# Hybrid conv / mLSTM / GLA trunk: three VectorE instructions placed behind the second head's key step

## The chip, the cores and the metric

The kernel runs on one core of one Trainium2 chip. The metric is device time in microseconds (us). The core has TensorE (PE) for matrix products, VectorE (DVE) and ScalarE (ACT) for elementwise work, GpSimd (POOL), and SyncE (SP), whose queue issues the DMAs here. Each engine works through its own list of instructions in order; a semaphore holds an instruction until what it reads is there.

## The reference

A trunk of two residual layers on a 1024 x 1024 activation (sequence x width), each followed by a dense SwiGLU, with a final RMSNorm. The change lies in the first layer's mixer, which is a causal 31-tap convolution module and a four-head mLSTM side by side:

```python
def conv_mlstm_mixer(h, w_in, conv_w, conv_b, ln_g, ln_b, qk_conv_w, qk_conv_b, gate_b, head_g, w_out):
    z = h @ w_in
    ca, cg, q, k, v, og, gates = jnp.split(z, cuts, -1)
    u = causal_depthwise_conv(ca * sigmoid(cg), conv_w, conv_b)     # 31 taps, 512 channels
    u = silu(layernorm(u, ln_g, ln_b))                              # over the 512 channels
    qk = silu(causal_depthwise_conv(concat([q, k]), qk_conv_w, qk_conv_b))   # 4 taps
    hm = mlstm_chunkwise(q, k, v, i_pre, f_pre)                     # 4 heads of 128
    hm = head_rmsnorm(hm * sigmoid(og), head_g)
    return concat([u, hm]) @ w_out

# one chunk of a head:
    S = (qc @ kc.T) * exp(logD - m_t)
    num = S @ vc + w_inter * (qc @ C);  den = S.sum(-1) + w_inter * (qc @ n)
    wk = exp(g - m_new) * kc
    C = decay * C + wk.T @ vc;  n = decay * n + wk.sum(-2)
```

The change touches the mean of `layernorm` over the convolution's output `u`, and the step `wk` of the second head.

## The kernel before

Activations lie feature-major, as eight tiles of 128 features by 512 positions for each half of the sequence. Every large product is done in three passes of TensorE: each fp32 operand is split into a high part, which ScalarE writes as a rounded copy (`wH`, `hH`), and a low part, which VectorE writes as the difference (`wL`, `hL`, line 168 for a mixer's weights); `mm3` (lines 174 to 176) then adds low x high, high x low and high x high into one PSUM bank. So a weight block of 128 x 1024 costs one DMA from SP (line 164, into one of two `raw` buffers), one ScalarE copy (line 167) and one VectorE subtraction (line 168). Without the last one its products can't start, and its `raw` buffer doesn't come free.

The first mixer is written as a list of steps, `ORDER0`. What matters here is its middle: `v3` (the fourth convolution), `a1a` and `x1a` (the second head's first half, prepared and mixed), `l` (layer norm), `g2` (value and output-gate products of the third head), `q2` (its query and key products).

- `conv(3)` ends with two VectorE additions (line 418) that take two convolution results `xy_289` and `xy_290` out of PSUM.
- `head_pre(1, 0)` is `a1a`. TensorE forms keys x queries (line 601) and transposes the keys (line 606). VectorE multiplies the scores by the decay, `rb` (line 612), scales the queries (line 613) and writes the weighted keys `kw` (line 615).
- `head_mix(1, 0)` is `x1a`. For each pair of chunks TensorE multiplies `kw` by the values (line 633), `rb` by the values (line 634) and, from the second chunk on, the queries by the running state `st` (line 636). VectorE writes that state: the first chunk's is a copy (line 639), the later ones are line 642. Then come the denominators (lines 647 to 649) and the division (line 652).
- `layer_norm()` adds the eight convolution tiles one after the other into `s` (line 434 once, line 436 six times), folds `s` in three shorter additions (line 428) and has TensorE average it with a matrix of constants (line 429). The rest of the norm takes that mean off all eight tiles (line 441), squares, sums, averages again and scales.
- `head_vo(2)` is `g2`: eight products per head, one per 128 positions, into banks `mm_2512`, `mm_2539`, `mm_2566` and so on, 24 matmuls of 256 columns each. VectorE takes the value half out (line 560) and ScalarE the gate half (line 561).
- `q2` is the loop's `"q"` branch. It asks for two weight blocks; the first one's low part is `wL_2733`.

The steps are not run in the order they are written. A planner keeps only the dependences, a priority for each instruction (`high_priority` moves weights and loads ahead) and its own estimate of each duration, and from these it sets one fixed order for each engine's list. The helper `behind(a, b)` gives the planner one more dependence: `a` may not stand ahead of `b`. It carries no semaphore, so on one engine it moves places in a list and adds no wait of its own. `made` holds the two instructions, high copy and low subtraction, of the weight block that was asked for last.

Of the kernel before, what the change touches and what calls it, by code (L numbers as in the profile page):

```python
# [13 lines left out]
ALU = mybir.AluOpType  # L14
PSUM = bass.MemoryType.PSUM

P = 128
# [64 lines left out]
def trunk_kernel(ctx, tc, xT, cols, gate_b0, ev_vo0, ev_u, ev_cw, ev_out, od_v0, od_u, od_out, gate_w2, fin_row,  # L82
                 w13, w2, out, xsp, rowd, ud, zd, ad, x1, cd, cv, td, vd, yd, bd, md):
    nc = tc.nc
    PE, ACT, DVE, POOL, SP = nc.tensor, nc.scalar, nc.vector, nc.gpsimd, nc.sync
# [10 lines left out]
    def nm(s):  # L96
        uid[0] += 1
        return f"{s}_{uid[0]}"

    def bank(tag):  # L100
        return ps.tile([P, 512], F32, tag=tag, name=nm(tag))

    def tmp(dt=F32):
        return tp.tile([P, HALF], dt, tag="t", name=nm("t"))
# [47 lines left out]
    def behind(ins, other):  # L152

        tc.add_manual_dep(ins.ins, other.ins.name, mybir.DependencyInfo(mybir.DependencyClass.NoSync, mybir.DependencyReason.DATA))


    made = []

    def weights(src, n, lo, off=WOFF, pool=None):

        own = {} if pool is None else {"bufs": 1}
        with tc.high_priority(offset=off):
            raw = wp.tile([P, 1088], F32, tag="raw", name=nm("raw"), bufs=2)[:, :n]
            SP.dma_start(raw, src)
            hi = (pool or wp).tile([P, 1088 if pool is None else n], F32R, tag="wH", name=nm("wH"), **own)[:, :n]
            low = (pool or wp).tile([P, 1088 if pool is None else n], F32R, tag="wL", name=nm("wL"), **own)[:, :n]
            first = ACT.activation(hi, raw, AF.Copy)
            cuts = lo.tensor_tensor(out=low, in0=raw, in1=hi, op=ALU.subtract)  # L168
        made[:] = first, cuts
        return hi, low  # L170
# [123 lines left out]
    def mixer0(cut, then):  # L294
        with tc.tile_pool(name="m0", bufs=1, reuse_waits="tile") as mp:
# [6 lines left out]
            def nextw(lo):  # L302
                return ready.pop(0) if ready else weights(ev_u[next(unit)], 1024, lo)
# [117 lines left out]
            Y = []  # L421

            def by_phase(t):
                return t.rearrange("p (e n) -> p e n", e=GT)

            def mean(b, s):
                for n in (4 * NT, 2 * NT, NT):
                    DVE.tensor_tensor(out=s[:, :n], in0=s[:, :n], in1=s[:, n:2 * n], op=ALU.add)
                PE.matmul(b, ones_p, s[:, :NT], start=True, stop=True)

            def layer_norm():

                s = tp.tile([P, HALF], F32, tag="s", name=nm("s"), bufs=1)
                DVE.tensor_tensor(out=s, in0=Y[0], in1=Y[1], op=ALU.add)
                for y in Y[2:]:
                    DVE.tensor_tensor(out=s, in0=s, in1=y, op=ALU.add)
                mu = bank("sm")[:, :NT]
                mean(mu, s)
                s = tp.tile([P, HALF], F32, tag="s", name=nm("s"), bufs=1)
                for j, y in enumerate(Y):  # L440
                    DVE.tensor_tensor(out=by_phase(y), in0=by_phase(y), in1=mu.unsqueeze(1).to_broadcast([P, GT, NT]),
                                      op=ALU.subtract)
                    t = tmp() if j else s
                    ACT.activation(t, y, AF.Square)
                    if j:
                        DVE.tensor_tensor(out=s, in0=s, in1=t, op=ALU.add)
                var = bank("sm")[:, :NT]
                mean(var, s)
                r = tp.tile([P, HALF], F32, tag="r", name=nm("r"), bufs=1)[:, :NT]
                rsqrt(r, var)  # L450
                for j, y in enumerate(Y):
                    DVE.tensor_tensor(out=by_phase(y), in0=by_phase(y), in1=r.unsqueeze(1).to_broadcast([P, GT, NT]), op=ALU.mult)
                    for e in range(0, GT, 4):
                        SP.dma_start(zd[GT * j + e:GT * j + e + 4].rearrange("e c a n -> (c a) e n"), by_phase(y)[:, e:e + 4])
# [14 lines left out]

                split(d, features[k, half], DVE, after)  # L470

            gcols = {}

            def gates(gz):

# [114 lines left out]
            def head_pre(hd, half, q, k):  # L590

                rb = mp.tile([P, HALF], F32, tag="bc0", name=nm("rb"), bufs=2)
                wb = mp.tile([P, HALF], F32, tag="bc1", name=nm("wb"), bufs=2)
                hs = slice(half * HALF, (half + 1) * HALF)
                SP.dma_start(rb, rowd[0, hd, hs].partition_broadcast(P))
                SP.dma_start(wb, rowd[1, hd, hs].partition_broadcast(P))
                cc, wk = gcols["c"], gcols["wk"]
                sb = bank("sm")
                for c in range(4):
                    cs = slice(c * P, (c + 1) * P)  # L600
                    PE.matmul(sb[:, cs], k[:, cs], q[:, cs], start=True, stop=True)
                kb = bank("sm")
                n = 4 - half
                for c in range(n):
                    cs = slice(c * P, (c + 1) * P)
                    PE.transpose(kb[:, cs], k[:, cs], ident)
                d3 = rb.rearrange("p (c t) -> p c t", c=4)
                DVE.tensor_tensor(out=d3, in0=d3, in1=mask.unsqueeze(1).to_broadcast([P, 4, P]), op=ALU.add)
                for c in range(4):
                    ci = half * 4 + c  # L610
                    ACT.activation(d3[:, c, :], d3[:, c, :], AF.Exp, bias=cc[:, ci, hd:hd + 1], scale=1.0)
                DVE.scalar_tensor_tensor(out=rb, in0=sb, scalar=SCALE, in1=rb, op0=ALU.mult, op1=ALU.mult)
                DVE.tensor_tensor(out=q, in0=q, in1=wb, op=ALU.mult)
                kw = mp.tile([P, HALF], F32, tag="kw", name=nm("kw"), bufs=KB)
                DVE.tensor_tensor(out=kw.rearrange("p (c t) -> p c t", c=4)[:, :n],
                                  in0=kb.rearrange("p (c t) -> p c t", c=4)[:, :n],
                                  in1=wk[:, half * 4:half * 4 + n, hd:hd + 1].to_broadcast([P, n, P]), op=ALU.mult)
                return q, rb, wb, kw

            def head_mix(hd, half, pre, v, og, st):  # L620
# [37 lines left out]
            def rnorm(hd, n, half):  # L658
                a = ssq[:, half * 16 + hd * 4:half * 16 + (hd + n) * 4]
                ACT.activation(a, a, AF.Sqrt, bias=epsc, scale=1.0 / P)  # L660
                DVE.reciprocal(a, a)
# [22 lines left out]
            for what in ORDER0:  # L684
                n = int(what[1]) if len(what) > 1 else 0
                halves = ["ab".index(what[2])] if len(what) > 2 else range(2)
                if what[0] == "l":
                    layer_norm()
                elif what[0] == "c":
                    conv_in(n)  # L690
                elif what[0] == "v":
                    conv(n)
                elif what[0] == "g":
                    heads[n]["v"], heads[n]["o"] = head_vo(n)
                    ogs.append(heads[n]["o"])
                elif what[0] == "q":
                    w = nextw(DVE), nextw(DVE)
                    for half in range(2):
                        for which in range(2):
                            heads[n][which, half], heads[n]["z", which] = head_qk(  # L700
                                n, which, half, w[which], heads[n]["z", which] if half else None)
                elif what[0] == "x":
                    for half in halves:
                        pre = heads[n].get(("p", half)) or head_pre(n, half, heads[n][0, half], heads[n][1, half])
                        heads[n]["s"] = head_mix(n, half, pre, heads[n]["v"], heads[n]["o"], heads[n]["s"] if half else None)
                elif what[0] == "a":
                    for half in halves:
                        heads[n]["p", half] = head_pre(n, half, heads[n][0, half], heads[n][1, half])
                elif what[0] == "z":
                    with tc.high_priority(offset=ZPR):  # L710
                        for half in range(2):
                            for k in range(4):
                                conv_silu(k, half)
                elif what[0] == "n":
                    for half in halves:
                        rnorm(0 if n == 3 else 3, n, half)
                else:
                    with tc.high_priority(offset=-CKP):
                        cut(get, 0, CUT0[n])
# [1309 lines left out]
```

## Time and profile before

| | |
|---|---|
| time, median of 3 runs | 2088.71 us (2087.4 to 2090.43) |
| the profiled execution's own time | 2089.46 us |
| span in its trace, first to last instruction | 2087.5 us |
| TensorE busy | 2068.3 us, 99% of the span |
| VectorE busy | 1491.1 us, 71% |
| ScalarE busy | 880.5 us, 42% |
| mean granted TensorE clock | 0.997 |

The span leaves 1.96 us of the profiled execution's time outside. Views used below: the waits of TensorE (who waited for whom, total us, times, longest us), the timeline (start us, duration us, engine, line, operation, out<-in, shapes, count, and in brackets the idle time of the engine just before and what ended it), and a table of stretches (us, then busy time and instruction count of each engine, then the granted TensorE clock as a share of full, the DMA share and GB/s). Instructions of one engine overlap a little: the next starts before the one ahead has ended, so the step from start to start is the cost in a row of instructions, and the duration counts only for the last. A matmul of fp32 operands is recorded as two.

### The profile page before, as it was taken

The page shows a single profiled execution, that of the slowest core. Times are in us where ns is not written, and L with a number is a line of the kernel's source. Part 1 is how long each engine was busy: PE and PEld are TensorE (multiplying, and loading weights), DVE is VectorE, ACT ScalarE, POOL GpSimd, SP SyncE. Part 2 cuts the span into 40 slices and gives each one's busy share as a digit, 9 for nine tenths or more (in the row PEclk, how much of TensorE's full clock was granted, in tenths as well). Part 3 has the DMA queues.
Part 4 walks back from the last instruction along what each step waited for, and adds up shares of the span by engine and source line. Part 5 has one row for each costly group of instructions (what it writes and reads, how often), then busy time and mean ns, then how long its engine had stood idle before and what let it go on. Part 6 is the DMA issues. An engine that isn't in the chain of part 4 may idle for free.

```text
span 2087.5 us, 28620 instructions
## 1 busy us (share of the span) xinstructions
PE 2068.3 (99%) x10799; PEld 1749.5 (84%) x10799; DVE 1491.1 (71%) x2269; ACT 880.5 (42%) x1418; POOL 3.8 (0%) x17
## 2 busy tenths in 40 slices
PE   9999999999999999999999999999999999999998
PEld 7888888888888888888899988888888888888887
DVE  7745787687775766877875677667887665777686
ACT  6421365453222222444646556644522232235553
POOL 0000000000000000000000000000000000000000
PEclk9999999999999999999999999999999999999999
DMA  4344254554443334734436643453644332384344
GB/s 158 100 120 129 80 127 152 197 185 171 156 143 102 106 106 163 251 107 147 145 125 234 201 138 129 162 202 131 207 156 166 110 113 101 101 283 136 96 127 147
DMA packets 168718, 308.43 MB, mean 148 GB/s; under 512 B 48448, under 2 KB 53440, under 8 KB 168576
## 3 DMA queue, kind: packets, MB, share of 16 engines
q1 hardware_dynamic: 168304, 306.30, 44.7%
q8 instruction: 86, 1.41, 0.3%
q14 instruction: 56, 0.46, 0.1%
q10 hardware_dynamic: 272, 0.26, 0.0%
HBM read 225.73 MB, written 80.77 MB: 147 GB/s over the span
## 4 chain that ended last, share of the span: by engine, by line
PE 96%; ACT 1%; DVE 1%; DMA 0%; issue 0%; SPq 0%; DVEq 0%; ACTq 0%
PE mm L174 21%; PE mm L175 21%; PE mm L176 21%; PE sm L175 10%; PE sm L176 10%; PE sm L174 10%; PE sm L1303 1%; PE sm L1302 1%; PE sm L1305 1%; DVE wL L168 0%; PE sm L412 0%; PE sm L1291 0%; PE sm L1333 0%; PE sm L634 0%; PE sm L633 0%
## 5 line engine op out<-in xcount | busy, mean ns | idle before, releaser
L175 PE MATMUL mm<-hL,wH 128*128 128x512 f32 x1356 | 530.6, 391 | 0.2 <-DVE hL L339 0.2
L176 PE MATMUL mm<-hH,wH 128*128 128x512 f32 x1356 | 528.6, 390 | 0.0
L174 PE MATMUL mm<-hH,wL 128*128 128x512 f32 x1356 | 493.6, 392 | 2.9 <-ACT hH L338 1.4
L174 PEld LDWEIGHTS mm<-hH,wL 128*128 128x128 f32 x1356 | 254.4, 188 | 57.6 <-ACT hH L338 2.6
L175 PEld LDWEIGHTS mm<-hL,wH 128*128 128x128 f32 x1356 | 254.7, 188 | 53.4 <-DVE hL L339 1.0
L176 PEld LDWEIGHTS mm<-hH,wH 128*128 128x128 f32 x1356 | 254.6, 188 | 52.9 <-issue 0.2
L175 PE MATMUL sm<-hL,wH 128*128 128x512 f32 x616 | 240.1, 390 | 0.0
L176 PE MATMUL sm<-hH,wH 128*128 128x512 f32 x616 | 239.7, 389 | 0.0
L174 PE MATMUL sm<-hH,wL 128*128 128x512 f32 x616 | 209.0, 390 | 0.0
L147 ACT ACTIVATE wH<-S 128x1024 fp32r<-128x1024 f32 x97 | 102.8, 1060 | 228.1 <-PE sm L176 214.4
L147 ACT ACTIVATE wH<-q 128x512 fp32r<-128x512 f32 x143 | 90.3, 632 | 178.7 <-PE mm L176 101.2
L147 DVE TENSOR_TENSOR wL<-q,wH 128x512 fp32r<-128x512 f32 x143 | 98.5, 689 | 71.3 <-ACT wH L147 70.9
L147 ACT ACTIVATE wH<-raw 128x1024 fp32r<-128x1024 f32 (+1 forms) x90 | 90.0, 1001 | 120.3 <-PE sm L176 66.8
L147 DVE TENSOR_TENSOR wL<-S,wH 128x1024 fp32r<-128x1024 f32 x97 | 118.4, 1221 | 28.6 <-ACT wH L147 28.6
L174 PE MATMUL mm<-wH,hL 128*128 128x256 f32 (+2 forms) x480 | 136.5, 287 | 0.1
L176 PE MATMUL mm<-wH,hH 128*128 128x256 f32 (+2 forms) x480 | 136.5, 286 | 0.0
L175 PE MATMUL mm<-wL,hH 128*128 128x256 f32 (+2 forms) x480 | 136.5, 286 | 0.0
L175 PEld LDWEIGHTS sm<-hL,wH 128*128 128x128 f32 x616 | 115.6, 188 | 24.6 <-issue 0.7
L174 PEld LDWEIGHTS sm<-hH,wL 128*128 128x128 f32 x616 | 115.7, 188 | 24.4 <-PE mm L176 0.5
L176 PEld LDWEIGHTS sm<-hH,wH 128*128 128x128 f32 x616 | 115.7, 188 | 24.3 <-issue 0.2
L1533 DVE TENSOR_TENSOR c<-sm,c 128x512 f32<-128x512 f32 x110 | 75.5, 687 | 71.9 <-PE sm L176 71.9
L147 DVE TENSOR_TENSOR wL<-raw,wH 128x1024 fp32r<-128x1024 f32 (+1 forms) x90 | 103.3, 1149 | 10.8 <-ACT wH L147 10.8
(356 smaller groups left out, 3521.0 us busy)
## 6 DMA issues: line engine op xcount, KB each, us to landing
raw<-in_w SPq DMA_DIRECT2D x108, 512.0 KB, 3.6
mdT<-c SPq DMA_DIRECT2D x88, 256.0 KB, 2.0
m<-mdT SPq DMA_DIRECT2D x88, 256.0 KB, 2.6
mdB<-c SPq DMA_DIRECT2D x66, 256.0 KB, 2.6
raw<-in_od_u SPq DMA_DIRECT2D x32, 512.0 KB, 3.9
q<-in_w SPq DMA_DIRECT2D x60, 256.0 KB, 5.3
m<-mdB SPq DMA_DIRECT2D x55, 256.0 KB, 2.7
raw<-in_ev_u SPq DMA_DIRECT2D x20, 512.0 KB, 3.4
```

The costliest lines, as they stand in the source:

```text
L147: ins = ACT.activation(dst[0], src, AF.Copy), lo.tensor_tensor(out=dst[1], in0=src, in1=dst[0], op=ALU.subtract)
L174: return (PE.matmul(o, lt[1], rt[0], start=start and not on, stop=False, skip_group_check=on), PE.matmul(o, lt[0], rt[1], start=False, sto ...
L175: PE.matmul(o, lt[0], rt[1], start=False, stop=False, skip_group_check=on),
L176: PE.matmul(o, lt[0], rt[0], start=False, stop=stop, skip_group_check=on))
L1302: PE.matmul(db[:, cc, :], kw[:, cs], v[:, c, :], start=True, stop=True)
L1303: PE.matmul(ob[:, cc, :], A[:, cs], v[:, c, :], start=True, stop=st is None)
L1305: PE.matmul(ob[:, cc, :], q[:, cs], st, start=False, stop=True)
L1533: DVE.tensor_tensor(out=out, in0=a, in1=b, op=ALU.add)
```

## The change

Three VectorE instructions get a further dependence, each on `kws[1, 0]`, the instruction that writes `kw` for the second head's first half (line 615): the fifth and sixth of layer norm's six accumulating additions (line 436, those of `xy_289` and `xy_290`), and the subtraction for the low part of the first weight block of `q2`. No instruction is added or taken away, no shape is changed, and no tile gets another buffer.

```diff
--- before.py
+++ after.py
@@ -432,8 +432,10 @@
 
                 s = tp.tile([P, HALF], F32, tag="s", name=nm("s"), bufs=1)
                 DVE.tensor_tensor(out=s, in0=Y[0], in1=Y[1], op=ALU.add)
-                for y in Y[2:]:
-                    DVE.tensor_tensor(out=s, in0=s, in1=y, op=ALU.add)
+                for j, y in enumerate(Y[2:]):
+                    ins = DVE.tensor_tensor(out=s, in0=s, in1=y, op=ALU.add)
+                    if j >= 4:
+                        behind(ins, kws[1, 0])
                 mu = bank("sm")[:, :NT]
                 mean(mu, s)
                 s = tp.tile([P, HALF], F32, tag="s", name=nm("s"), bufs=1)
@@ -469,7 +471,7 @@
 
                 split(d, features[k, half], DVE, after)
 
-            gcols = {}
+            gcols, kws = {}, {}
 
             def gates(gz):
 
@@ -612,9 +614,9 @@
                 DVE.scalar_tensor_tensor(out=rb, in0=sb, scalar=SCALE, in1=rb, op0=ALU.mult, op1=ALU.mult)
                 DVE.tensor_tensor(out=q, in0=q, in1=wb, op=ALU.mult)
                 kw = mp.tile([P, HALF], F32, tag="kw", name=nm("kw"), bufs=KB)
-                DVE.tensor_tensor(out=kw.rearrange("p (c t) -> p c t", c=4)[:, :n],
-                                  in0=kb.rearrange("p (c t) -> p c t", c=4)[:, :n],
-                                  in1=wk[:, half * 4:half * 4 + n, hd:hd + 1].to_broadcast([P, n, P]), op=ALU.mult)
+                kws[hd, half] = DVE.tensor_tensor(
+                    out=kw.rearrange("p (c t) -> p c t", c=4)[:, :n], in0=kb.rearrange("p (c t) -> p c t", c=4)[:, :n],
+                    in1=wk[:, half * 4:half * 4 + n, hd:hd + 1].to_broadcast([P, n, P]), op=ALU.mult)
                 return q, rb, wb, kw
 
             def head_mix(hd, half, pre, v, og, st):
@@ -694,7 +696,10 @@
                     heads[n]["v"], heads[n]["o"] = head_vo(n)
                     ogs.append(heads[n]["o"])
                 elif what[0] == "q":
-                    w = nextw(DVE), nextw(DVE)
+                    w = [nextw(DVE)]
+                    if n == 2:
+                        behind(made[1], kws[1, 0])
+                    w.append(nextw(DVE))
                     for half in range(2):
                         for which in range(2):
                             heads[n][which, half], heads[n]["z", which] = head_qk(
```
On VectorE, at the end of the fourth convolution and the second head's first half (`xy_289` and `xy_290` are the last two convolution tiles, `s_2320` is layer norm's sum, `wL_2733` is the low part of the first `q2` weight, `kw_2275` is the second head's weighted keys, `st_2281` its first state, `v_2506` the third head's values). Before:

```order
L418 TENSOR_TENSOR xy_290_2252<-sm_2145,col 128x512
L168 TENSOR_TENSOR wL_2733<-raw_2730,wH_2732 128x1024
L436 TENSOR_TENSOR s_2320<-s_2320,xy_289_2250 128x512
L612 SCALAR_TENSOR_TENSOR rb_2254<-sm_2258,rb_2254 128x512
L613 TENSOR_TENSOR qk_2032<-qk_2032,wb_2255 128x512
L615 TENSOR_TENSOR kw_2275<-sm_2263,wk 128x512
L436 TENSOR_TENSOR s_2320<-s_2320,xy_290_2252 128x512
L428 TENSOR_TENSOR s_2320<-s_2320 128x256
L428 TENSOR_TENSOR s_2320<-s_2320 128x128
L428 TENSOR_TENSOR s_2320<-s_2320 128x64
L560 TENSOR_SCALAR v_2506<-mm_2512,rt 128x128
L639 COPY st_2281<-sm_2277 128x129
```
With the change (the lines after the edits are numbered two to five higher in places):

```order
L418 TENSOR_TENSOR xy_290_2252<-sm_2145,col 128x512
L614 SCALAR_TENSOR_TENSOR rb_2254<-sm_2258,rb_2254 128x512
L615 TENSOR_TENSOR qk_2032<-qk_2032,wb_2255 128x512
L617 TENSOR_TENSOR kw_2275<-sm_2263,wk 128x512
L436 TENSOR_TENSOR s_2320<-s_2320,xy_289_2250 128x512
L168 TENSOR_TENSOR wL_2733<-raw_2730,wH_2732 128x1024
L436 TENSOR_TENSOR s_2320<-s_2320,xy_290_2252 128x512
L428 TENSOR_TENSOR s_2320<-s_2320 128x256
L562 TENSOR_SCALAR v_2506<-mm_2512,rt 128x128
L641 COPY st_2281<-sm_2277 128x129
L428 TENSOR_TENSOR s_2320<-s_2320 128x128
L428 TENSOR_TENSOR s_2320<-s_2320 128x64
```
The three steps that end in `kw_2275` now follow the convolution's two additions directly; the subtraction and the first of the two layer-norm additions, which stood ahead of them, stand behind. The shorter fold of `s` is now interleaved with the value copy and the state copy.

On TensorE, at the border between the first two products of `g2` (`mm_2512` and `mm_2539`). Before, the end of the second group's first five matmuls and the second head's products behind them:

```order
L174 MATMUL mm_2539<-wH_2496,hL_28_158 128x256
L175 MATMUL mm_2539<-wL_2497,hH_27_157 128x256
L633 MATMUL sm_2277<-v_1654,kw_2275 128x129
L634 MATMUL sm_2278<-v_1654,rb_2254 128x129 x2
L633 MATMUL sm_2298<-v_1654,kw_2275 128x129
L634 MATMUL sm_2299<-v_1654,rb_2254 128x129
L176 MATMUL mm_2539<-wH_2496,hH_27_157 128x256
L174 MATMUL mm_2539<-wH_2496,hL_30_162 128x256
L175 MATMUL mm_2539<-wL_2497,hH_29_161 128x256
L176 MATMUL mm_2539<-wH_2496,hH_29_161 128x256
```
With the change, the end of `mm_2512`:

```order
L175 MATMUL mm_2512<-wL_2503,hH_39_181 128x256
L176 MATMUL mm_2512<-wH_2502,hH_39_181 128x256
L635 MATMUL sm_2277<-v_1654,kw_2275 128x129
L636 MATMUL sm_2278<-v_1654,rb_2254 128x129 x2
L635 MATMUL sm_2298<-v_1654,kw_2275 128x129
L636 MATMUL sm_2299<-v_1654,rb_2254 128x129
L174 MATMUL mm_2539<-wH_2496,hL_26_154 128x256
L175 MATMUL mm_2539<-wL_2497,hH_25_153 128x256
L176 MATMUL mm_2539<-wH_2496,hH_25_153 128x256
L174 MATMUL mm_2539<-wH_2496,hL_28_158 128x256
```
The five products with `kw_2275` and `rb_2254` have moved ahead of five matmuls of `mm_2539`. Later the next products of this head, with line 633 and line 636, stand three matmuls of `mm_2539` earlier, and those that end in line 429 three matmuls of `mm_2566` earlier.

On SP, fifty microseconds further on, where the queue loads normalised convolution tiles (`zt`), the third and fourth heads' rows (`rb`, `wb`) and weights (`raw`). Before:

```order
L596 DMA wb_3093<-rowd 128x512
L462 DMA zt_2470<-zd 128x16x32
L164 DMA raw_3188<-in_ev_u 128x1024
L595 DMA rb_3092<-rowd 128x512
L462 DMA zt_2474<-zd 128x16x32
L462 DMA zt_2478<-zd 128x16x32
```
With the change:

```order
L598 DMA wb_3093<-rowd 128x512
L464 DMA zt_2470<-zd 128x16x32
L597 DMA rb_3092<-rowd 128x512
L164 DMA raw_3188<-in_ev_u 128x1024
L464 DMA zt_2474<-zd 128x16x32
L464 DMA zt_2478<-zd 128x16x32
```
The row `rb_3092` and the weight block `raw_3188` have changed places. Around the same place VectorE and ScalarE each exchange a few neighbours. POOL's list is the same, and behind this mixer no list differs.

## The prediction

> **What bounds the kernel now.** The page first: the share of busy time, and the chain of work that ended last.
>
> ```profile
> PE 2068.3 (99%) x10799; PEld 1749.5 (84%) x10799; DVE 1491.1 (71%) x2269; ACT 880.5 (42%) x1418; POOL 3.8 (0%) x17
> PE 96%; ACT 1%; DVE 1%; DMA 0%; issue 0%; SPq 0%; DVEq 0%; ACTq 0%
> ```
>
> TensorE sets the time. So a change in VectorE's order can pay only where TensorE stands still or runs slowly. The waits of TensorE are the next view:
>
> ```profile
> PE sm L633 <- DVE kw L615: 3.1, 1, 3.1
> PE sm L412 <- DMA cw<-in_ev_cw: 1.8, 1, 1.8
> ```
>
> The longest wait of the whole span is one wait for `kw`, the instruction that the change moves. The second, in the convolution, the change doesn't touch; it serves as a yardstick below. TensorE's timeline around the wait (`mm` rows of one kind between those shown are left out):
>
> ```profile
> 218.87 0.28 PE L174 MATMUL mm<-wH,hL 128*128 128x256 f32 x1
> ...
> 219.35 0.28 PE L175 MATMUL mm<-wL,hH 128*128 128x256 f32 x1
> 222.69 0.80 PE L633 MATMUL sm<-v,kw 128*128 128x129 f32 x2 [3.06 <-DVE kw L615]
> ...
> 224.86 0.56 PE L176 MATMUL mm<-wH,hH 128*128 128x256 f32 x1
> ...
> 228.21 0.62 PE L633 MATMUL sm<-v,kw 128*128 128x129 f32 x2
> ...
> 228.81 0.36 PE L176 MATMUL mm<-wH,hH 128*128 128x256 f32 x1
> ...
> 231.52 0.38 PE L636 MATMUL sm<-st,qk 128*128 128x129 f32 x2
> ...
> 232.55 0.36 PE L174 MATMUL mm<-wH,hL 128*128 128x256 f32 x1
> ```
>
> From 218.87 to 219.35 the five matmuls of `mm_2539` step by 0.12 us, so the last one's slot ends at 219.47 and the standstill is 222.69 - 219.47 = 3.22 us. Behind it the work doesn't run at its usual pace. The table of stretches says why (columns: stretch, its length and TensorE's busy time, weight loads, VectorE, ScalarE, POOL, granted clock, DMA share, GB/s):
>
> ```profile
> 184.33:187.74 3.41, 1.86 (x99) 1.59 (x97) 2.33 (x4) 3.05 (x4) 0.00 (x0) 1.00 0.59 217
> 218.47:221.88 3.41, 1.16 (x10) 0.96 (x8) 2.96 (x5) 0.51 (x1) 0.00 (x0) 1.00 0.49 163
> 221.88:225.29 3.41, 2.60 (x12) 2.60 (x13) 2.76 (x8) 0.37 (x1) 0.00 (x0) 0.50 0.27 103
> 225.29:228.70 3.41, 3.41 (x18) 3.41 (x18) 0.00 (x0) 0.00 (x0) 0.00 (x0) 0.50 0.00 0
> ```
>
> From 221.88 to 228.70 the granted clock is a half. It was cut after a stretch in which TensorE was busy for 1.16 of 3.41 us; the yardstick's stretch, 1.86 busy of 3.41, kept its clock. So the wait costs twice: the standstill, and 6.82 us at half clock, of which 222.69 to 228.70 has work.
>
> **VectorE's side.** Its timeline, with what ScalarE gives it:
>
> ```profile
> 217.29 1.28 DVE L418 TENSOR_TENSOR xy<-sm,col 128x512 f32<-128x512 f32 x2
> 219.01 1.22 DVE L168 TENSOR_TENSOR wL<-raw,wH 128x1024 fp32r<-128x1024 f32 x1 [0.45 <-ACT wH L167]
> 220.16 0.68 DVE L436 TENSOR_TENSOR s<-s,xy 128x512 f32<-128x512 f32 x1
> 220.76 0.68 DVE L612 SCALAR_TENSOR_TENSOR rb<-sm,rb 128x512 f32<-128x512 f32 x1
> 221.36 0.68 DVE L613 TENSOR_TENSOR qk<-qk,wb 128x512 f32<-128x512 f32 x1
> 221.96 0.68 DVE L615 TENSOR_TENSOR kw<-sm,wk 128x512 f32<-128x512 f32 x1
> 222.56 0.68 DVE L436 TENSOR_TENSOR s<-s,xy 128x512 f32<-128x512 f32 x1
> 223.27 1.01 DVE L428 TENSOR_TENSOR s<-s 128x256 f32<-128x256 f32 x3
> 224.20 0.34 DVE L560 TENSOR_SCALAR v<-mm,rt 128x128 f32<-128x128 f32 x1
> 224.46 0.28 DVE L639 COPY st<-sm 128x129 f32<-128x129 f32 x1
> 228.87 0.81 DVE L642 SCALAR_TENSOR_TENSOR st<-st,wb,sm 128x129 f32<-128x129 f32 x2 [4.13 <-PE sm L633]
> 217.40 0.63 ACT L587 ACTIVATE qk<-qk 128x512 f32<-128x512 f32 x1 [3.63 <-DVE qk L585]
> 217.94 1.04 ACT L167 ACTIVATE wH<-raw 128x1024 fp32r<-128x1024 f32 x1
> ```
>
> Between the convolution's additions (done at 219.01 - 0.45 = 218.56) and line 612 stand 0.45 of waiting for the high part of a weight, the subtraction (1.15 from start to start) and one layer-norm addition (0.60): 2.20 us. Nothing of this is needed by line 612: its scores come from TensorE's line 601, done long before. `kw` ends at 221.96 + 0.68 = 222.64, and TensorE goes on 0.05 later.
>
> **Part 1, the standstill.** With the change line 612 starts at 218.56, line 613 at 219.16, line 615 at 219.76, which ends at 220.44; TensorE goes on at 220.49, 2.20 earlier. But in TensorE's list the products have also moved ahead of the five matmuls, so TensorE stops 5 x 0.12 = 0.60 sooner, at 218.87. The standstill becomes 220.49 - 218.87 = 1.62 us, a gain of 3.22 - 1.62 = 1.60 us. The five matmuls are not lost; they count in part 2's sum.
>
> **Part 2, the clock.** With 1.62 us of standstill no stretch of 3.41 us has less than 1.79 us of work, against 1.86 where the clock was kept and 1.16 where it was cut. I take it as kept. What the same instructions take at full clock the fourth head's twin stretch shows:
>
> ```profile
> 296.70 0.38 PE L633 MATMUL sm<-v,kw 128*128 128x129 f32 x2
> ...
> 297.73 0.36 PE L174 MATMUL mm<-wH,hL 128*128 128x256 f32 x1
> 297.94 0.28 PE L175 MATMUL mm<-wL,hH 128*128 128x256 f32 x1
> ...
> 300.08 0.38 PE L633 MATMUL sm<-v,kw 128*128 128x129 f32 x2
> ...
> 300.44 0.36 PE L175 MATMUL mm<-wL,hH 128*128 128x256 f32 x1
> ```
>
> The five products take 1.03 us there (297.73 - 296.70), 2.17 here (224.86 - 222.69): 1.14 lost. Then 15 matmuls: here 228.21 - 224.86 = 3.35; there the first takes 0.21 and the 18 to 300.08 take 0.119 each, so 0.21 + 14 x 0.119 = 1.88: 1.47 lost. The pair of lines 633 and 636: 0.60 here, 0.36 there: 0.24 lost. Sum 2.85 us, which fits 6.01 us at half clock (about 3.0). Its bounds: nothing gained, if 1.62 us still cuts the clock; 2.85, if it doesn't.
>
> [...]
>
> **Part 3, what is late next.** The moved subtraction and addition now stand between `kw` and the state copy (line 639), which the next product with `st` (line 636) needs. VectorE: line 436 at 220.36, the subtraction at 220.96 (its high part is done at 218.98), line 436 at 222.11, the fold at 222.82 (0.71 later, as from 222.56 to 223.27), of which one instruction now stands ahead of line 560; the three take 0.93 together, the first is the longest, I take 0.5 (0.31 to 0.93). Line 560 at 223.32, the copy at 223.58 (0.26), ready at 223.86 + 0.05 = 223.91. TensorE: 220.49 + 1.03 = 221.52, then 17 matmuls (three fewer than the 20 of before) 0.21 + 16 x 0.119 = 2.11, line 633 at 223.63, line 636 at 223.85. That is 0.06 us of waiting, 0.4 at the worst: I take nothing off. Line 642 has the 4.13 us of idle time before it as cover. The fold ends by about 224.3, and line 429 reads it behind 22 more matmuls.
>
> To the end of the stretch: 223.63 + 0.36 + 2.71 (231.52 - 228.81, 22 matmuls) + 1.03 (232.55 - 231.52) + 3 x 0.12 for the three matmuls that line 429 has passed = 228.09, against 232.55: 4.46 us, which is parts 1 and 2 (1.60 + 2.85 = 4.45).
>
> The low part itself is for `q2`, whose products stand behind all of `g2`'s. Its `raw` buffer comes free at 222.11 instead of 220.16; the next block loaded into it gets its high part in the first of these rows:
>
> ```profile
> 247.94 1.06 ACT L167 ACTIVATE wH<-raw 128x1024 fp32r<-128x1024 f32 x1 [0.38 <-PE mm L176]
> 270.60 2.32 SPq L164 DMA_DIRECT2D raw<-in_ev_u  x1
> 273.01 0.38 SPq L595 DMA_DIRECT2D rb<-rowd  x1
> 293.50 1.05 ACT L167 ACTIVATE wH<-raw 128x1024 fp32r<-128x1024 f32 x1
> ```
>
> That is 25 us of cover (and ScalarE waits there for a product to free its target): no cost. The two DMAs that change places on SP's queue are the second and third row here; the weight's own cut, the fourth, has 20 us in hand, and the `rb` row is used by products from 296.70 on: no cost. Without cover, the weight would be late by the rb row's 0.38 us.
>
> **The sum** against the profiled execution: 2089.46 - 1.60 - 2.85 = 2085.01 us. That execution is 0.75 us above the median of the runs; I read the difference as clock loss that the median run had less of (the three runs spread over 3.03 us, near the 2.85 that the clock costs), so the gain on the median is 3.7 us: **2085.0 us**, 0.18% below 2088.71. What a measurement of this kernel can tell from no change is 0.2%, 4.18 us, so a time under 2084.53: the likeliest verdict is no measurable difference, from below.
>
> **The rivals.**
>
> A, the forecast, chance 0.60, own range 2084.0 to 2086.2; about 0.16 of it lies below 2084.53.
>
> B, the clock part isn't there to be gained, 0.16: the new 1.62 us still cuts the clock (1.79 us of work lies a little under the 1.86 that kept it), or typical runs were never cut. Then only part 1 is left: 2088.71 - 1.60 = 2087.1. For it: the shortest of the runs, 2087.4. Against: the cut in the one trace. [...]
>
> C, the typical run loses the whole 2.85 and the 0.75 is something else, 0.15: 2088.71 - 4.45 = 2084.3; some 0.11 of it below 2084.53.
>
> D, the wait moves to the state copy, 0.04: the fold's 0.93 wholly ahead of it and a little more, 0.7 us late. Two idle pieces of 1.62 and 0.7 in one stretch come to the 2.25 (3.41 - 1.16) that was cut, so the clock part goes too: 2085.0 + 0.7 + 2.85 = 2088.5.
>
> E, slower, 0.05: the subtraction waits on VectorE for its high part, now with the state copy behind it. ScalarE gives it at 218.98, the subtraction asks at 220.96, so the first 1.98 us of lateness are free. From 0.7 us more the clock goes as in D; from 1.6 more all is lost (1.6 + 2.85 = 4.45); to be 0.2% slower the high part must be 1.98 + 5.8 = 7.8 us late, for a time of 2092.9. Against it: the high part began at 217.94, right behind line 587 (the row above it), so its load was there.
>
> The range that holds 8 in 10 reaches into B and C: 2083.4 to 2087.5. Faster by over 0.2%: 0.16 + 0.11 = 0.27; slower: 0.05; within: 0.68.
>
> **What would show it.** Right: TensorE's wait for `kw` falls from 3.1 to about 1.6 us; the table of stretches shows clock 1.00 throughout here; the five products follow in 1.03 us; no wait of line 636 for line 639 over 0.4. Wrong: a row of 0.50 clock behind the wait (B), a new wait of line 636 (D), idle time before the moved subtraction (E), or a `kw` that starts later than 219.9 because line 612 waits for something that the queue had hidden.

## The result, and the profile after

| | before | with the change |
|---|---|---|
| median of 22 runs each | 2089.23 us | 2085.28 us |
| lowest to highest | 2086.78 to 2090.65 | 2084.19 to 2088.43 |
| the profiled execution's own time | 2089.46 us | 2084.83 us |
| its span | 2087.5 us | 2083.0 us |

The ratio is 0.9984, with a 95% interval of 0.9977 to 0.999: 0.16% faster, about 3.3 us, or 3.95 us by the medians. By the interval the gain is between 2.1 and 4.8 us. It is clear of no change and, as a point, inside the 0.2% that was set as the bound.

The lines after the edits are numbered two to five higher, so `kw` is line 617, the products are lines 635, 636 and 638. The waits of TensorE in the changed kernel:

```profile
PE sm L412 <- DMA cw<-in_ev_cw: 1.6, 1, 1.6
PE sm L635 <- DVE kw L617: 1.4, 1, 1.4
```

The wait for `kw`, longest of all before (3.1), is now behind the convolution's. TensorE's timeline of the changed kernel shows where it stops and goes on:

```profile
218.91 0.28 PE L176 MATMUL mm<-wH,hH 128*128 128x256 f32 x1
220.58 0.49 PE L635 MATMUL sm<-v,kw 128*128 128x129 f32 x2 [1.39 <-DVE kw L617]
...
221.72 0.36 PE L174 MATMUL mm<-wH,hL 128*128 128x256 f32 x1
...
223.83 0.49 PE L635 MATMUL sm<-v,kw 128*128 128x129 f32 x2
224.16 0.39 PE L638 MATMUL sm<-st,qk 128*128 128x129 f32 x2
```

The first product's last matmul starts at 218.91, its slot ends 0.12 later, and TensorE goes on at 220.58: a standstill of 1.55 us against 3.22. The five products take 1.14 us (221.72 - 220.58) against 2.17. VectorE's timeline:

```profile
217.45 1.28 DVE L418 TENSOR_TENSOR xy<-sm,col 128x512 f32<-128x512 f32 x2
218.65 0.68 DVE L614 SCALAR_TENSOR_TENSOR rb<-sm,rb 128x512 f32<-128x512 f32 x1
219.24 0.68 DVE L615 TENSOR_TENSOR qk<-qk,wb 128x512 f32<-128x512 f32 x1
219.84 0.68 DVE L617 TENSOR_TENSOR kw<-sm,wk 128x512 f32<-128x512 f32 x1
220.44 0.68 DVE L436 TENSOR_TENSOR s<-s,xy 128x512 f32<-128x512 f32 x1
221.04 1.21 DVE L168 TENSOR_TENSOR wL<-raw,wH 128x1024 fp32r<-128x1024 f32 x1
...
223.50 0.28 DVE L641 COPY st<-sm 128x129 f32<-128x129 f32 x1
```

The three steps to `kw` follow the convolution's additions at once, the moved subtraction starts with no idle time before it, and the state copy ends at 223.78, before line 638 at 224.16. The table of stretches, laid so that the whole standstill falls into the first one:

```profile
217.65:221.07 3.42, 2.03 (x17) 1.83 (x17) 3.42 (x7) 1.49 (x2) 0.00 (x0) 1.00 0.47 161
221.07:224.48 3.41, 3.41 (x30) 3.37 (x30) 3.22 (x9) 0.37 (x1) 0.00 (x0) 1.00 0.36 105
224.48:227.89 3.41, 3.41 (x31) 3.41 (x30) 1.67 (x8) 1.12 (x6) 0.00 (x0) 1.00 0.12 49
```

TensorE's busy time in the first stretch is 2.03 us, against 1.16 before, and the granted clock (the third number from the end) stays at 1.00 behind the standstill, where it was 0.50 before.

One distance sums up the place: from `g2`'s first matmul, the first of 256 columns, to `q2`'s first, of 512 columns. TensorE's timeline of the kernel before, and then of the changed one:

```profile
215.91 0.36 PE L174 MATMUL mm<-wH,hL 128*128 128x256 f32 x1
...
247.74 0.40 PE L174 MATMUL mm<-hH,wL 128*128 128x512 f32 x1
```

```profile
216.07 0.36 PE L174 MATMUL mm<-wH,hL 128*128 128x256 f32 x1
...
243.59 0.40 PE L174 MATMUL mm<-hH,wL 128*128 128x512 f32 x1
```

31.83 us has become 27.52: 4.31 us gone. The two spans differ by 4.5 us (2087.5 against 2083.0), so the gain is nearly all here. From `q2`'s first matmul to the output projection's first (328.92 before, 324.77 after, by the same timelines) it is 81.18 us in both: the DMAs and the neighbours that changed places further on moved nothing in these two executions.

### The profile page after: what moved, and what is told of

Same layout as the page of the kernel before. It is cut to its first block, busy times and chain, and to the rows that moved or that the text cites. A ratio compares the mean times of both kernels' runs of the same rounds, so it can differ in the third digit from the quotient of the medians.

```text
span 2083.0 us, 28618 instructions
## 1 busy us (share of the span) xinstructions
PE 2066.6 (99%) x10799; PEld 1748.0 (84%) x10799; DVE 1491.6 (72%) x2269; ACT 880.7 (42%) x1418; POOL 3.8 (0%) x17
## 3 DMA queue, kind: packets, MB, share of 16 engines
q8 instruction: 86, 1.41, 0.3%
## 4 chain that ended last, share of the span: by engine, by line
PE 97%; DVE 1%; ACT 1%; DMA 0%; issue 0%; SPq 0%; DVEq 0%; ACTq 0%
PE mm L174 21%; PE mm L175 21%; PE mm L176 21%; PE sm L174 10%; PE sm L176 10%; PE sm L175 10%; PE sm L1308 1%; PE sm L1307 1%; PE sm L1310 1%; PE sm L412 0%; PE sm L1296 0%; DVE wL L168 0%; PE sm L1338 0%; PE sm L636 0%; PE sm L603 0%
```

## The experiments

Theory 1 is that of the prediction: TensorE's standstill costs twice, as idle time and as a clock cut behind it. Theory 2: only the idle time costs, and the half clock in the one trace was chance. The window of the expectations is a stretch of 3.41 us, as in the tables; that the clock goes by it was the author's assumption. Each experiment was run beside the kernel before on the same chip; ratios are to that, with 95% intervals. The distance from `g2`'s first matmul to `q2`'s first is read from each profile as above.

| run | wait for `kw`, us | clock behind it | distance, us | ratio to before |
|---|---|---|---|---|
| before | 3.1 | half for 6.83 us | 31.83 | |
| before, another execution (e11) | 3.6 | half for 6.83 us | 32.13 | |
| the change | 1.4 | full | 27.52 | 0.9984 (0.9977 to 0.999) |
| the change again (e5) | 1.4 | full | 27.53 | 0.9982 (0.9973 to 0.9991) |
| only the weight moved (e1) | 2.4 | half for 3.41 us | 30.04 | 0.9992 (0.9983 to 1.0) |
| only the sums moved (e2) | 2.8 | half for 3.41 us | 30.42 | 0.9994 (0.9985 to 1.0003) |
| the change, `kw` twice (e3) | 2.2 | half for 3.41 us | 29.73 | 0.9988 (0.998 to 0.9997) |
| the change, `kw` four times (e4) | 3.7 | half for 3.41 us | 31.19 | 1.0004 (0.9995 to 1.0013) |
| the change, products later (e6) | none | full | 25.76 | 0.9984 (0.9975 to 0.9993) |
| before, products later (e7) | none | full | 25.77 | 0.9985 (0.9976 to 0.9994) |
| before, useless work ahead of `g2` (e8) | 3.1 | half for 3.41 us | 35.19 | 1.0019 (1.001 to 1.0028) |
| the change, useless work (e9) | 1.4 | full | 29.07 | 0.9993 (0.9984 to 1.0002) |
| before, useless work in the standstill (e10) | none | full | 29.69 | 0.9999 (0.999 to 1.0008) |

In e8 and e9 the distance counts from the first useless matmul.

**Each half of the change alone.** e1 keeps only the weight's dependence, e2 only that of the sums.

```diff
 # e1
-                    if j >= 4:
-                        behind(ins, kws[1, 0])
 # e2
-                    if n == 2:
-                        behind(made[1], kws[1, 0])
```

> Only the weight's low part is held behind kw; layer norm's additions are free again. VectorE's list now has both additions of line 436 ahead of line 612 and the first fold (line 428) ahead of kw. From the rows of the kernel before: additions of line 418 done at 218.56, line 436 at 218.56 and 219.27, line 612 at 219.87, line 613 at 220.47, the fold at 221.07, kw from about 221.42 to 222.10, TensorE on at 222.15. Theory 1 (standstill plus clock): TensorE's wait falls from 3.2 to about 2.7 us, still long enough to cut the clock in most executions, so 0.5 to 1.5 us faster than the kernel before. Rival (the weight's place alone makes the gain): 3.4 us faster or more, wait 1.6 us.

> Only layer norm's two additions are held behind kw; the weight's low part is free again and stands ahead of line 614 as before. The wait for the high part (0.45) and the subtraction stay in front: line 614 at 220.16, kw from 221.36 to 222.04, TensorE on at 222.09; two matmuls of the second product stand ahead, so the standstill is 222.09 - 219.11 = 2.98 us. Theory 1: 0.2 to 0.8 us faster than the kernel before, the clock still cut at half for 3.4 to 6.8 us in most executions. Rival (the additions' place alone makes the gain): 3.4 us faster.

Neither alone brings most of the gain. VectorE's timeline of e1 shows what filled the freed place:

```profile
216.71 1.28 DVE L418 TENSOR_TENSOR xy<-sm,col 128x512 f32<-128x512 f32 x2
217.91 1.41 DVE L436 TENSOR_TENSOR s<-s,xy 128x512 f32<-128x512 f32 x2
219.24 0.68 DVE L612 SCALAR_TENSOR_TENSOR rb<-sm,rb 128x512 f32<-128x512 f32 x1
219.84 0.68 DVE L613 TENSOR_TENSOR qk<-qk,wb 128x512 f32<-128x512 f32 x1
220.44 0.42 DVE L428 TENSOR_TENSOR s<-s 128x256 f32<-128x256 f32 x1
220.77 0.69 DVE L615 TENSOR_TENSOR kw<-sm,wk 128x512 f32<-128x512 f32 x1
```

With the weight gone the planner put both layer-norm additions and a fold ahead of `kw` (1.33 and 0.33 us from start to start), so `kw` gains little. In e2 the subtraction and its wait for the high part stay in front. Both distances lie under the one before, by 1.79 and 1.41 us. The waits are only 0.7 and 0.3 us shorter; the rest goes with the shorter cut of the clock, 3.41 us at half clock instead of 6.83. By the ratios they are 1.7 and 1.3 us faster, a little above theory 1's ranges. Both intervals reach to about no change, and that of e1 also to the 3.4 us of its rival, so it is the profiles that speak against the rivals: neither half alone brought the wait near the change's 1.4 us or kept the clock.

**The standstill put back.** In e3 and e4 the changed kernel writes `kw` two and four times with the same values, and the second product of `g2` is held behind the five products, so that the planner can't fill the time.

```diff
-                kws[hd, half] = DVE.tensor_tensor(
+                for _ in range(2 if (hd, half) == (1, 0) else 1):      # e4: 4
+                    kws[hd, half] = DVE.tensor_tensor(
...
+            if after is not None and k == 0:       # after: the last of the five products
+                behind(ms[0], after)
```

> The changed kernel with kw written twice (the same values) and the second product of g2 held behind the five products, so that the planner can't fill the time: the standstill is 0.60 us longer than the changed kernel's, about 2.15 us. Theory 1: 0.6 us slower than the changed kernel if the clock is kept, up to 3.4 us slower where it is cut; since 2.25 us of idle time in one window did cut it, I expect a cut in some executions: 0.6 to 2 us slower than the changed kernel, 2.0 to 3.4 us faster than the kernel before. Theory 2 (only the standstill costs, the half clock in the one trace was chance): 0.6 us slower than the changed kernel.

> As the run before it, with kw written four times: the standstill is about 3.35 us, a little more than in the kernel before (3.22), while the order of VectorE and TensorE is that of the change. Theory 1: the standstill costs 1.8 us and the clock is cut again in most executions, 1.7 to 2.9 us: 3.5 to 4.7 us slower than the changed kernel, so the kernel before's time within 1 us. Theory 2: 1.8 us slower than the changed kernel, 1.6 to 2.2 us faster than the kernel before.

TensorE's waits and its table of stretches, of e3 and then of e4:

```profile
PE sm L638 <- DVE kw L620: 2.2, 1, 2.2
218.39:221.80 3.41, 1.34 (x12) 1.14 (x10) 3.38 (x7) 1.41 (x2) 0.00 (x0) 1.00 0.46 156
221.80:225.21 3.41, 3.27 (x15) 3.31 (x16) 3.38 (x7) 0.37 (x1) 0.00 (x0) 0.50 0.20 59
```

```profile
PE sm L638 <- DVE kw L620: 3.7, 1, 3.7
220.36:223.78 3.42, 0.70 (x6) 0.73 (x7) 3.32 (x6) 0.00 (x0) 0.00 (x0) 1.00 0.00 0
223.78:227.19 3.41, 3.41 (x18) 3.41 (x18) 2.89 (x7) 0.37 (x1) 0.00 (x0) 0.50 0.46 147
```

e3's distance is 2.2 us longer than the changed kernel's for 0.8 us more of waiting; the half clock of 3.41 us costs the other 1.4. Its time, 2.5 us faster than the kernel before, fits both theories. e4 lost the whole gain: against the changed kernel, 1.0004 to 0.9984, it is 4.2 us slower, inside theory 1's 3.5 to 4.7. Its repeats step by 0.69 us, not 0.60 (why was not tested), so the wait came out 2.3 us longer than the changed kernel's instead of 1.8. By the wait alone the kernel would then be about 1 us faster than before, a ratio of 0.9995, which is the edge of the interval: the time speaks for theory 1, and the profile decides it, 3.67 us more of distance for 2.3 us more of waiting.

**The standstill taken away without VectorE.** e6 is the changed kernel and e7 the kernel before, both with a lower priority for the second head's mixing step, which moves the products back in TensorE's list. e5 is the changed kernel beside them.

```diff
+                        with tc.high_priority(offset=-140 if (n, half) == (1, 0) else 0):    # e7: -160
                             heads[n]["s"] = head_mix(...)
```

> The changed kernel itself, beside the next two on the same chip: 3 to 4 us faster than the kernel before, TensorE's wait for kw 1.4 to 1.6 us, no half clock in the stretch behind it.

> The changed kernel, with the second head's mixing step of this half given a lower priority, so that TensorE's list has its first product behind 27 matmuls of the second and third products of g2 instead of ahead of all of them. Theory (the standstill and the clock are all there is): the wait for kw is gone, 1.4 to 1.6 us faster than the changed kernel, 4.5 to 5.5 us faster than the kernel before. Rival (the products' results, or layer norm's mean behind them, are needed soon): the wait comes back behind line 429 or at the next head, and the time is the changed kernel's or longer.

> The kernel before, VectorE's order untouched, with the same lower priority a little stronger: TensorE's list has the first product behind 47 matmuls of the second and third products of g2, that is at about 218.87 + 47 x 0.119 = 224.5, when kw (ready at 222.64) has long been written. Theory (only TensorE's standstill and clock count, not VectorE's order): no wait for kw, the clock kept, the same time as the run before it, 4.5 to 5.5 us faster than the kernel before. Rival (VectorE's order itself is what gains): no faster than the kernel before by more than 1 us.

TensorE's timeline of e7, and one stretch from `g2`'s first matmul to `q2`'s first:

```profile
223.99 0.28 PE L175 MATMUL mm<-wL,hH 128*128 128x256 f32 x1
224.11 0.38 PE L633 MATMUL sm<-v,kw 128*128 128x129 f32 x2
215.50:241.30 25.80, 25.80 (x220) 25.80 (x219) 21.60 (x48) 12.26 (x32) 0.00 (x0) 1.00 0.22 76
```

The wait is gone in both, the clock full, and both distances are 25.8 us, though e7 has VectorE's old order. So at this place the order on VectorE is worth nothing by itself; what counts is that TensorE doesn't come to the products before `kw` is written.

TensorE is busy here from end to end at full clock, so 25.77 us is what the work alone takes, and it prices the other runs without useless matmuls, which have the same 216 matmul records in this stretch. The kernel before is 6.06 us longer; its standstill of 3.22 leaves 2.84 us for the clock; with 3.72 in e11 it is 2.64. The changed kernel is 1.75 us longer, its standstill of 1.55 and 0.20 for a slower start behind it. By the same working, with standstills of 2.61, 2.99, 2.36 and 3.81 us, the cut of 3.41 us costs 1.6 to 1.7 us in e1, e2, e3 and e4.

In time both e6 and e7 miss what was expected of them: they are as fast as the changed kernel (0.9984 and 0.9985 against 0.9982), not 1.5 us faster. For e7 the profile shows a new wait that took part of it:

```profile
PE sm L601 <- DVE st L642: 1.3, 1, 1.3
```

Behind the query and key products, at 298.56, TensorE waits at a line 601, which it doesn't in the kernel before. To the output projection e7 needs 108.64 us from `g2`'s first matmul, the changed kernel 108.70. e6 needs 107.23, and its span is 2081.2 us, but the medians (2084.54 against 2084.28 for e5) don't show it, and intervals of 0.18% can't separate 1.5 us. Whether e6 is a better kernel stays open.

**The clock by itself.** If theory 1 holds, useless matmuls in the standstill should keep the clock, with `kw` as late as ever. e8 and e9 put them at the start of the mixing step, ahead of the products:

```diff
+                if (hd, half) == (1, 0):
+                    pad = bank("mm")
+                    for i in range(27):          # e9: 13, in the changed kernel
+                        ins = PE.matmul(pad[:, :256], h[0][i % 8][0][:, :P], h[0][i % 8][0][:, P:3 * P], start=True, stop=True)
```

> The kernel before with VectorE's order untouched. TensorE gets 27 useless matmuls (256 columns, 0.12 us each, 3.2 us in all, into a spare turn of an mm bank that nobody reads) ahead of g2's first product, about as much as the standstill; the planner then puts the second head's products behind two matmuls of the second product instead of five. kw is as late as before (222.6 us into the old time), so TensorE gets no further: the useless work fills the standstill, wait for kw about 0.5 us, and three matmuls (0.36 us) are left for later. Theory 1 (the standstill cuts the clock): no half clock in the stretch behind it, 2.85 us less in an execution like the profiled one, so 1 to 2.5 us faster than the kernel before, from g2's start (useless work counted) to q2's first matmul about 31.83 - 2.85 + 0.36 = 29.3 us. Theory 2 (the half clock is chance or has another cause): 0.4 us slower than the kernel before, 32.2 us.

> The changed kernel with 13 such useless matmuls (1.55 us) in the same place. The planner now puts the second head's products 13 matmuls earlier among g2's, so TensorE stops for kw at the same time as before. Theory 1: there is no clock to save in the changed kernel, so the useless work only costs its time: 1.5 us slower than the changed kernel, 1.5 to 2.5 us faster than the kernel before; from g2's start to q2's first matmul 27.5 + 1.55 = 29.1 us. Theory 2 (useless work ahead of a wait helps by itself): no slower than the changed kernel.

e8 missed, and by its own fault. Its expectation took the product that follows the useless matmuls in TensorE's list for the second of `g2`; it is the first. The planner had made room by letting the products overtake the real work. TensorE's timeline of e8:

```profile
215.09 3.48 PE L626 MATMUL mm<-hH 128*128 128x256 f32 x27
221.87 0.80 PE L639 MATMUL sm<-v,kw 128*128 128x129 f32 x2 [3.07 <-DVE kw L615]
```

The standstill is as long as before, the clock is cut behind it, and the useless 3.2 us are added: 0.19% slower, 4.0 us. The distance of 35.19 can't be set beside the others: 1.2 us of it are products of line 601 and line 606 that stand behind `q2`'s first matmul in the other lists. e9 came out as theory 1 said (a distance of 29.07 for 29.1, and by the ratio 1.5 us faster than before, with an interval that reaches no change): without a cut to save, useless work only costs its time.

e10 does it rightly. `g2`'s first product is written ahead of the mixing step, 32 useless matmuls are held behind it, and the first product with `kw` behind these; VectorE's order is that of the kernel before.

```diff
+                early.append(proj_tok(*early, 256, h, 0, 0, pads))
+                pad = bank("mm")
+                for i in range(32):
+                    ins = PE.matmul(pad[:, :256], ...)
+                    behind(ins, pads[-1])
+                    pads.append(ins)
...
+                            if hd == 1 and ci == 0:
+                                behind(ins, pads[-1])
```

> The kernel before, VectorE's order untouched, and now the useless matmuls stand inside the standstill: TensorE's list has g2's first product (24 matmuls), 32 useless matmuls of 256 columns (0.119 us each, 3.8 us), then the second head's products; the five matmuls of the second product that stood ahead of them come later (0.60 us). kw is as late as in the kernel before, so nothing useful moves forward. Theory 1 (the idle window cuts the clock): wait for kw under 0.5 us, no half clock behind it, and from g2's first matmul to q2's first 31.83 - 2.6 + 0.6 = 29.8 us; against the kernel before 1 to 2 us faster, and no execution with a clock cut at this place. Theory 2 (the half clock is chance or has another cause): 31.83 + 0.6 = 32.4 us there, 0.6 us slower than the kernel before.

> The kernel before, profiled in another execution. Theory 1: TensorE waits 3.1 us for kw again, and the clock is cut behind it again, for 3.4 or 6.8 us according to where the edge of the window falls. Theory 2: no half clock at this place this time.

TensorE's timeline and the table of stretches of e10:

```profile
216.96 0.36 PE L174 MATMUL mm<-wH,hL 128*128 128x256 f32 x1
...
219.92 4.00 PE L551 MATMUL mm<-hH 128*128 128x256 f32 x32
223.76 0.48 PE L649 MATMUL sm<-v,kw 128*128 128x129 f32 x2
...
246.65 0.40 PE L174 MATMUL mm<-hH,wL 128*128 128x512 f32 x1
```

```profile
219.00:223.70 4.70, 4.70 (x42) 4.70 (x40) 4.25 (x8) 1.03 (x2) 0.00 (x0) 1.00 0.59 200
223.70:228.70 5.00, 5.00 (x44) 4.97 (x44) 3.34 (x12) 0.56 (x3) 0.00 (x0) 1.00 0.04 14
```

The first product with `kw` starts 6.80 us behind `g2`'s first matmul, as in the kernel before (222.69 - 215.91 = 6.78), and five real matmuls fewer are done by then. Still `q2` begins after 29.69 us instead of 31.83: 2.14 us less for 3.8 us of useless work, with a clock that isn't cut here (1.00 from 219.00 to 228.70). That is theory 1's 29.8, and theory 2's 32.4 is excluded for this execution. The time missed the 1 to 2 us that were expected: 0.9999 with an interval of 0.18% holds 1 us faster as well as 0.6 slower, so it speaks for neither theory.

e11 is the kernel before once more. Its waits and its table of stretches:

```profile
PE sm L633 <- DVE kw L615: 3.6, 1, 3.6
PE sm L412 <- DMA cw<-in_ev_cw: 2.0, 1, 2.0
```

```profile
185.28:188.69 3.41, 1.42 (x96) 1.31 (x92) 2.38 (x3) 2.13 (x2) 0.00 (x0) 1.00 0.75 262
188.69:192.10 3.41, 3.41 (x31) 2.71 (x21) 2.58 (x4) 0.00 (x0) 0.00 (x0) 0.50 0.89 274
219.41:222.82 3.41, 1.09 (x10) 0.89 (x8) 2.46 (x5) 0.94 (x1) 0.00 (x0) 1.00 0.38 127
222.82:226.24 3.42, 2.17 (x11) 2.18 (x11) 3.19 (x8) 0.29 (x1) 0.00 (x0) 0.50 0.38 137
226.24:229.65 3.41, 3.41 (x18) 3.41 (x18) 0.00 (x0) 0.08 (x1) 0.00 (x0) 0.50 0.00 0
```

The clock is cut behind the wait again, from 222.82 to 229.65, and this time behind the convolution's wait too, from 188.69 to 192.10. Over all profiles: seven with a wait for `kw` of 2.2 us or more, and the clock cut behind it in each; six with 1.4 us or none, and it is cut there in none.

## Why the prediction was right, step by step

- **Part 1, the standstill**: predicted 3.22 to 1.62, measured 3.22 to 1.55. Right; the steps of VectorE follow one another at 0.60 as read from the rows before.
- **Part 2, the clock**: predicted kept, with 2.85 us saved. It was kept, in both profiles of the changed kernel. Of the 4.31 us that went, 1.67 are the standstill, so 2.64 are left for the clock, 0.2 less than the twin stretch had promised. Beside e7's distance the cut itself cost 2.84 us, as forecast; the 0.20 stay with the changed kernel, half of them in the five products behind its standstill (1.14 us here, 1.03 there). The margin was wider than the forecast's 1.79 against 1.86: it counted the standstill by slots of 0.12 us, but the table counts each matmul to its recorded end, and by the table 2.03 us of work were left in the stretch with the standstill. A wait well below the old 3.1 us was followed by a cut all the same: 2.2 us in e3. That the clock goes by the work in a stretch of 3.41 us was an assumption of the forecast and isn't shown: the clock was kept behind a stretch with 1.55 us in e7 and cut behind one with 2.10 us early in the changed kernel (5.70 to 9.11).
- **Part 3, what is late next**: the copy was predicted to be ready at 223.91 with 0.06 us of waiting, 0.4 at the worst. It ended at 223.78, with all of this timeline 0.16 us later than the one before, and line 638 started 0.33 us behind line 635 where the twin stretch has 0.22: about 0.1 us. The two DMAs and the low part: no cost, 81.18 us on both sides.
- **The sum**: 2085.0 us predicted, 2085.28 measured. Against the profiled execution, 2085.01 predicted and 2084.83 measured. The step that took 0.75 us off for the median isn't settled: over these 22 runs the median of the kernel before, 2089.23, is only 0.23 under its profiled execution, but in the four samples of it beside the experiments (15 to 35 runs each) the median is 1.1 to 2.0 under. That the forecast came within 0.3 us is in part luck, since it started from a median 0.5 us lower and the interval of the gain is 2.7 us wide.
- **The rivals**: B is excluded for the cut (full clock in both profiles), and its other half, that typical runs were never cut, is spoken against by two cuts in two profiles of the kernel before, by five in five of the other long waits and by e4. D and E didn't come: no wait at line 638 worth the name, no idle time before the moved subtraction. C can't be told from the forecast by the times: with the larger sample its number would be 2089.23 - 4.45 = 2084.8, and the forecast's 2089.23 - 3.7 = 2085.5.
- **The verdict**: no difference over 0.2%, as the chances had it (0.68), but with an interval that reaches to 0.23%.

What the times alone can't show: how much a typical execution loses to the clock. That the two sides of the change are 1.67 and 2.64 us is shown by the profiles before and after; the median gain of 3.3 to 3.95 us is more than the first alone, as is the lower end of its interval, 2.1. Every run has its mean granted clock on record: 0.9981 on average over 98 runs of the kernel before beside the experiments, 0.9986 over 33 of the changed kernel. As an estimate from these, 0.0005 of 2086 us, a typical execution of the changed kernel loses about 1 us less to the clock, not 2.64.

## What to carry to other kernels

Where TensorE is busy 99% of the time, look at its longest single wait, and then at the granted clock behind it: the standstill of 3.2 us here cost 2.8 us more in the work that followed, where the cut lasted 6.83 us, and cuts half as long behind other standstills cost 1.6 to 1.7 us. Such a wait can be taken away on either side, by moving what stands ahead of the late instruction or by moving the waiting work back in TensorE's list; and a change that moves only one of two pieces of work ahead of the late instruction may gain little: in e1 the planner put other work there.

## What the runs showed of the hardware that was not expected

The clock was cut behind waits well under 3.41 us: 2.2 us for `kw` in e3, 1.9 us for `cw` in e5. In e11 two cuts start at 188.69 and 222.82, ten times 3.41 us apart. At the waits for `kw` and `cw` the cuts of the tables start behind stretches of 3.41 us with 0.70 (e4) to 1.48 us (e5) of TensorE work, and the clock was kept behind stretches with 1.55 (e7), 1.86 (before) and 2.03 us (the changed kernel). The tables of e5 and then of e7, both with a wait of 1.9 us for `cw`:

```profile
184.72:188.13 3.41, 1.48 (x100) 1.34 (x96) 2.67 (x4) 3.30 (x4) 0.00 (x0) 1.00 0.49 183
188.13:191.54 3.41, 3.41 (x98) 3.15 (x92) 1.00 (x3) 0.00 (x0) 0.00 (x0) 0.50 0.89 301
```

```profile
185.13:188.55 3.42, 1.55 (x108) 1.42 (x100) 2.70 (x3) 2.69 (x4) 0.00 (x0) 1.00 0.55 193
188.55:191.96 3.41, 3.41 (x64) 2.88 (x56) 2.58 (x4) 0.00 (x0) 0.00 (x0) 1.00 0.87 294
```

Two waits of the same 1.9 us came out differently. The busy time of a stretch alone doesn't say which way it goes: in the changed kernel the clock was also cut from 9.11 to 12.52, behind a stretch (5.70 to 9.11) with 2.10 us of work, and why stays open.

By the table's count the changed kernel is idle for 1.39 us, which leaves 2.02 us of work in a stretch of 3.41 us that holds all of it. The kernel before is idle for 3.06 us, and its clock was cut in both profiles; in what share of its executions was not shown.

A cut lasted 3.41 us where its first stretch held 3.27 (e3) or 3.41 us (e4) of work, and 6.83 us where it held 2.60 (the kernel before) or 2.17 us (e11). TensorE went on 0.81 us (before, 222.69 - 221.88) and 1.24 us (e11, 224.06 - 222.82) behind the start of the long cuts, 0.14 us behind that of e3 (221.94 - 221.80) and 0.70 us ahead of that of e4 (223.78 - 223.08), whose wait of 3.7 us brought only the short cut. These four agree with e11's expectation that the length depends on where the cut starts.
